# A hybrid encoder layer on one core: re-planned with a shared read port and measured step lengths, the last chunk's norms at once, first transfers in another sequence

## Chip, core and metric

One core of a Trainium2 chip runs one launch. The time is device time in microseconds of that core, 1225.96 us as the median of 3 runs of the kernel before. The engines are TensorE (PE; its weight loads are shown as PEld), VectorE (DVE), ScalarE (ACT), GpSimd (POOL) and SyncE (SP), which issues all transfers.

## The reference, cut to what matters

One layer is computed for 1024 prompt frames and 64 sample frames (1088 columns in all), with 1024 channels in f32. Only what carries time stands here.

```python
def _layer(h, ...):
    proj = _rmsnorm(h, pre_mix_g) @ w_in                     # 1024 x 2056
    z, xbc, dt_raw, u_pool = split(proj)
    xbc, new_conv = _causal_dwconv(xbc, conv_hist, conv_w, conv_b)   # width 4
    xs, bm, cm = split(silu(xbc))
    dt = softplus(dt_raw + dt_bias)
    y, new_ssm = _ssd_scan(xs, dt, -exp(a_log), bm, cm, ssm_h0)      # 8 heads
    y = (y + d_skip * xs) * silu(z)
    y = y * rsqrt(mean(y * y, per group) + EPS) * ssm_norm_g
    pool_out, new_pool = _multiscale_pool(u_pool, pool_hist, ...)    # windows 2, 4, 8, 16
    h = h + _rmsnorm(concat(y, pool_out) @ w_out, post_mix_g)
    hn = _rmsnorm(h, pre_ffn_g)
    f = (silu(hn @ w_gate) * (hn @ w_up)) @ w_down           # 2816 wide
    h = h + _rmsnorm(f, post_ffn_g)
    e = (p_i @ w_ple_proj) * sigmoid(h @ w_ple_gate)
    h = h + _rmsnorm(e, ple_norm_g)
```

## The kernel before, in words

The 1088 columns are cut into four chunks of 272 (`CH`, the last holds the sample frames too), and all activations lie with channels on the partitions. Each f32 operand of a large product is split into a high part rounded to fp32r (a cast on ACT) and a low part (the difference, on DVE, helper `sub`, L400); a product is then three fp32r matmuls of 272 columns: high x high, high x low, low x high (`PASSES`, helper `run`, L476). The stages follow each other on TensorE: the input projection with the convolution groups, the pooling groups and the gate (about 6 to 275 us), with the SSD scan's small matmuls in between; the output projection by chunks (to about 375); 32 small products of the per-layer input, the fills (372 to 401; L1801 is the ACT copy that frees their PSUM bank); the FFN in two phases, gate and up then down (401 to 1108, L1618); the input gate (to 1212); the tail. The FFN uses a seven-product block scheme: each operand exists in seven forms (`FORMS`), each form a cast on ACT (L1453, L1546) and a low part on DVE (L400). `hforms(p)` makes them for a pair of chunks p, from normed activations; `mixf` is the residual stream that it reads. A PSUM accumulation of the FFN ends in L1881 on DVE.

The order of all queues is written out by a planner while the program is built (`Layout`). Jobs are generators that yield a request: an engine letter, a length in us, and optionally a wait. "A" is ACT, "D" DVE, "G" POOL, "P" a small piece on TensorE, "S" SP. The planner keeps a time at which each engine comes free, gives the next place on an engine to the job that can start first (ties within 0.2 us by priority), and lets the clock run by the planned length of each matmul (`mmt`). TensorE's large products come in program order; the pieces "P" are put in where the planned time stands. A wait of 0, 1 or 2 means a hop of 0.2 us after the step before on another engine, TW means 0.04, and a number n from 3 on means n x 0.92 us. Transfers are planned at 500 or 680 columns per us. On the chip there is no planner: each engine runs its queue in order and waits on semaphores, so that a planned length only decides the order.

`rstd_job` (L497) makes 1/sqrt(mean + eps) for a chunk: eight one-column matmuls sum over the partitions (L511; twice the count in the trace's f32 passes), nine tiny DVE steps on 68 x 4 elements (L516 to L545) do the root, and four transposes bring the values back as a row in PSUM (L549):

```python
        f = 0 if fast else 1
        yield ("P", 0.52 * na, f)
        # L511, then L516 ("D", 0.16), then eight of ("D", 0.16, TW) up to L545
        yield ("P", 0.3 * na, 3 * f)
        # L549
```

`post_mix(c)` uses it twice for each output chunk: for the norm behind the output projection (tiles t_m), then `two(i)` scales pairs of channel blocks on DVE (L1402), adds x on POOL (L1408, `XM = 'GGGG'`) and squares (L601, sums L608 and L619), and again for the norm ahead of the FFN (tiles t_h), then `norm(m)` eight times on DVE (L1433). Neither was fast.

At the start, transfers are issued in this order: 8 parameter columns, the first half of input weight 0, x pieces of chunk 0 (piece 0), the dt weights (32 KB), the second half of weight 0, pieces 1 to 3, weight 1, the other 772 parameter columns (386 KB), weights 2 and 3, then chunk 1's pieces. A piece is two channel blocks k, 272 KB. `x_split` makes the high part on ACT (L731) and the low part on DVE (L733); `x_square` squares and adds for the norm, chunk 0 on POOL (L756). The first group of products runs by k (L914: high weight with both parts of x; L918: low weight). The dt products (L720) need `dt_w` (L815, L816) on DVE. `gt_job` (L841) multiplies four parameter columns on DVE; it is planned 10 x 0.92 us after the start, without a tie to the transfer:

```python
    def gt_job():
        yield ("D", 0.16, 10)
        ve.tensor_tensor(pcol("pool_b"), pcol("pool_b"), pcol("pool_scale"), ALU.mult)
```

## Time and profile before

| | |
|---|---|
| runs | 1224.27, 1225.96, 1226.66 us |
| profiled execution, its own time | 1226.61 us |
| its span, first to last instruction | 1224.8 us |
| mean granted TensorE clock | 0.993 |
| TensorE busy / weight loads | 1200.6 / 1180.8 us |
| DVE / ACT / POOL busy | 872.8 / 571.8 / 69.4 us |
| moved by DMA | 182.56 MB |

Times in the trace are microseconds from the first instruction. Busy time of TensorE counts matmuls as overlapping pipelines. An idle time is named by what released the engine; a wait on several semaphores is put down to the one that came last.

### The profile page before, as it was taken

Reading aid. Unit: us, or ns where it says so; the run is one execution under the profiler, and the core shown is the slowest. Engines: PE = TensorE matmul, PEld = TensorE weight load, DVE = VectorE, ACT = ScalarE, POOL = GpSimd, SP = SyncE. Lnnn points to the kernel's source line nnn. Section 1 sums busy time; section 2 is a strip of 40 time slices with the busy share of each in tenths; the row PEclk is TensorE's granted clock in tenths of the full one; section 3 lists DMA queues with packets and bytes.
Section 4 is the critical chain, followed back from the end, with each engine's and each line's share of the span. In section 5 each row is a group of like instructions: output and inputs, shape, how many; then the busy total and the mean of one; then the engine's idle time right before and its main releaser. Section 6 shows DMA issues by size and latency. Waiting matters only on the chain.

```text
span 1224.8 us, 23784 instructions
## 1 busy us (share of the span) xinstructions
PE 1200.6 (98%) x9641; PEld 1180.8 (96%) x9641; DVE 872.8 (71%) x1572; ACT 571.8 (47%) x1119; POOL 69.4 (6%) x56
## 2 busy tenths in 40 slices
PE   8999999999999999999999999999999999999997
PEld 6999999999999899999999999999999999999996
DVE  5697787874898776676677576766646655688875
ACT  6365557854456444443444444444432212356543
POOL 2000000120232000000000000000000000001111
PEclk8999999999999999999999999999999999999998
DMA  6122133243354144443443344336978676334422
GB/s 224 45 74 88 54 110 106 61 124 119 123 175 161 64 133 153 161 151 119 143 162 135 125 153 162 116 140 244 394 299 287 217 254 220 127 108 128 138 82 83
DMA packets 73777, 182.56 MB, mean 149 GB/s; under 512 B 8700, under 2 KB 17220, under 8 KB 73668
## 3 DMA queue, kind: packets, MB, share of 16 engines
q1 hardware_dynamic: 73668, 181.06, 42.9%
q8 instruction: 75, 1.23, 0.4%
q14 instruction: 34, 0.28, 0.1%
HBM read 122.03 MB, written 59.00 MB: 148 GB/s over the span
## 4 chain that ended last, share of the span: by engine, by line
PE 62%; DVE 3%; DMA 2%; POOL 0%; ACT 0%; issue 0%; DVEq 0%; ACTq 0%; POOLq 0%; SPq 0%
PE psall L1618 54%; PE psall L476 6%; PE psall L493 2%; DMA al_B<-af_dram 1%; POOL mixf L1408 0%; DMA raw_d<-in_wdn_dram 0%; DVE f L1881 0%; PE psall L511 0%; DMA raw_pg<-in_wpg_dram 0%; DVE mixf L1433 0%; DVE sq_f L608 0%; PE psall L549 0%; DMA e_dram<-e 0%; DVE mixf L1402 0%; DVE mixf L1465 0%
## 5 line engine op out<-in xcount | busy, mean ns | idle before, releaser
L476 PE MATMUL psall<-x,w_in 128*128 128x272 f32 x1440 | 193.8, 291 | 0.0
L476 PEld LDWEIGHTS psall<-x,w_in 128*128 128x128 f32 x1440 | 184.0, 188 | 3.3 <-issue 2.8
L1881 DVE TENSOR_TENSOR f<-f,psall 128x544 f32<-128x544 f32 (+1 forms) x96 | 60.7, 638 | 69.3 <-PE psall L1618 67.7
L1618 PE MATMUL psall<-h_T,w_g_S 128*128 128x272 f32 x792 | 102.9, 290 | 2.2 <-DVE h_T L400 1.8
L1618 PEld LDWEIGHTS psall<-h_T,w_g_S 128*128 128x128 f32 x792 | 101.1, 191 | 2.6 <-DVE h_T L400 2.0
L1618 PE MATMUL psall<-al_T,w_d_S 128*128 128x272 f32 x768 | 100.1, 289 | 1.0 <-ACT sq_f L601 0.5
L1618 PE MATMUL psall<-h_T,w_u_S 128*128 128x272 f32 x792 | 100.7, 287 | 0.0
L1618 PEld LDWEIGHTS psall<-h_T,w_u_S 128*128 128x128 f32 x792 | 99.6, 188 | 0.0
L1618 PEld LDWEIGHTS psall<-al_T,w_d_S 128*128 128x128 f32 x768 | 97.6, 188 | 1.7 <-ACT sq_f L601 0.7
L476 PE MATMUL psall<-mix,w_out 128*128 128x272 f32 x720 | 93.3, 289 | 0.0
L476 PEld LDWEIGHTS psall<-mix,w_out 128*128 128x128 f32 x720 | 90.9, 188 | 0.0
L1618 PE MATMUL psall<-al_B,w_d_A 128*128 128x272 f32 x528 | 72.1, 289 | 2.6 <-DVE w_d_A L400 2.6
L476 PE MATMUL psall<-h,w_pg 128*128 128x272 f32 x576 | 74.3, 289 | 0.0
L476 PEld LDWEIGHTS psall<-h,w_pg 128*128 128x128 f32 x576 | 72.7, 188 | 0.0
L1618 PEld LDWEIGHTS psall<-al_B,w_d_A 128*128 128x128 f32 x528 | 68.4, 188 | 3.1 <-DVE w_d_A L400 3.1
L1618 PE MATMUL psall<-h_B,w_g_A 128*128 128x272 f32 x528 | 70.2, 288 | 0.1
L1618 PE MATMUL psall<-h_B,w_u_A 128*128 128x272 f32 x528 | 69.7, 288 | 0.0
L1618 PEld LDWEIGHTS psall<-h_B,w_g_A 128*128 128x128 f32 x528 | 67.7, 188 | 0.3 <-ACT e L1801 0.3
L1618 PEld LDWEIGHTS psall<-h_B,w_u_A 128*128 128x128 f32 x528 | 67.5, 188 | 0.0
L1546 ACT CAST w_d_A<-raw_d 128x512 fp32r<-128x512 f32 (+3 forms) x44 | 22.3, 523 | 69.9 <-PE psall L1618 35.1
L1546 ACT CAST w_d_S<-raw_d 128x512 fp32r<-128x512 f32 (+3 forms) x54 | 26.5, 532 | 57.7 <-DVE raw_d L1570 33.9
L2067 POOL TENSOR_TENSOR f<-f,sq_f 128x544 f32<-128x544 f32 x5 | 7.4, 1479 | 726.8 <-DVE f L2064 721.3
(401 smaller groups left out, 2246.0 us busy)
## 6 DMA issues: line engine op xcount, KB each, us to landing
af_dram<-a_T SPq DMA_DIRECT2D x88, 272.0 KB, 2.3
al_T<-af_dram SPq DMA_DIRECT2D x44, 544.0 KB, 5.6
af_dram<-a_B SPq DMA_DIRECT2D x66, 272.0 KB, 2.2
al_B<-af_dram SPq DMA_DIRECT2D x33, 544.0 KB, 5.9
raw_g<-in_wff_dram SPq DMA_DIRECT2D x22, 512.0 KB, 4.1
raw_u<-in_wff_dram SPq DMA_DIRECT2D x22, 512.0 KB, 3.7
raw_in<-in_wmix_dram SPq DMA_DIRECT2D x15, 512.0 KB, 3.8
raw_d<-in_wdn_dram SPq DMA_DIRECT2D x14, 512.0 KB, 5.3
```

The source lines that it names most:

```text
L476: pe.matmul(out, lhsT, rhs, start=i == 0, stop=i == n - 1)
L493: pe.matmul(out, w.v(wi, k), act.v(xi, k, L), start=first and n == 0, stop=not left and n == 2)
L1546: ac.copy(v[:, 0], src)
L1618: pe.matmul(d[:, p - q.ps[0], :], w.v(wi, k), u.b(bf, xi, p, k), start=start and not k and not wi and not xi, stop=k == u.ks - 1 and wi == ...
L1881: ve.tensor_tensor(v[:, sl], v[:, sl], src[:, pl], ALU.add)
L2067: gp.tensor_tensor(v, v, hr, ALU.add)
```

## The change

Part 1: `FAST_M` and `FAST_H` name chunk 3, whose two calls of `rstd_job` in `post_mix` are now fast. Part 2: the first transfers. Chunk 0's pieces 0 and 1 stand between the halves of weight 0; the dt weights come behind all of chunk 0; chunk 1's pieces 0 and 1 come behind weight 1, and the parameters behind weight 2. Part 3: the planner has a new letter "E" for DVE steps that read two tensors in SBUF; E and G steps don't overlap in the plan. Steps get other lengths. `mmt` goes from 14 to 12 added columns, and a weight is given back after its own last group. `dma_add` and the branches for "A" are new, but no letter in `XM` or `XF` is "A" (`XM, XF = 'GGGG', 'GDGD'`).

```diff
+FAST_M, FAST_H = (3,), (3,)
...
+        self.port = {"E": 0.0, "G": 0.0}
...
-                if callable(req) or req[0] not in self.busy:
+                if callable(req) or req[0] not in "ADEG":
                     continue
-                start = max(job["ready"], self.busy[req[0]])
+                start = max(job["ready"], self.busy["D" if req[0] == "E" else req[0]])
+                if req[0] in "EG":
+                    start = max(start, self.port["G" if req[0] == "E" else "E"])
...
+            if eng in "EG":
+                self.port[eng] = start + cost
+            if eng == "E":
+                eng = "D"
...
-        return (1.0625 * n + 14) / 2400
+        return (1.0625 * n + 12) / 2400
...
-        xr0 += [x_dma(C0, k2) for k2 in ((0,), (1, 2, 3))[h]]
-        if not h:
-            dt_at = dma(wdr, wdt, NK * 8)
+        xr0 += [x_dma(C0, k2) for k2 in ((0, 1), (2, 3))[h]]
+    dt_at = dma(wdr, wdt, NK * 8)
...
-    dma(cp[:, PFIRST:], par[:, PFIRST:], PWIDTH - PFIRST)
+    xr1 = [x_dma(ORD_X[1], k2) for k2 in range(2)]
     for i in (2, 3):
+        if i == 3:
+            dma(cp[:, PFIRST:], par[:, PFIRST:], PWIDTH - PFIRST)
...
     def x_job():
+        for k2 in range(2):
+            x_spawn(ORD_X[1], k2, *xr1[k2], P_XP)
         for c in ORD_X[1:]:
-            for k2 in range(4):
+            for k2 in range(2 if c == ORD_X[1] else 0, 4):
...
             conv_group(i, c, getw(f"in{i}"), i == 0)
-    for i in range(4):
-        donew(f"in{i}")
+            if c == ORD_X[-1]:
+                donew(f"in{i}")
...
-        yield from rstd_job(ss.halves(), L, 1024.0, f"m{c}", flag, free=ss.free)
+        yield from rstd_job(ss.halves(), L, 1024.0, f"m{c}", flag, fast=c in FAST_M, free=ss.free)
...
-            yield from rstd_job(ss2.halves(), L, 1024.0, f"h{c}", got, free=ss2.free)
+            yield from rstd_job(ss2.halves(), L, 1024.0, f"h{c}", got, fast=c in FAST_H, free=ss2.free)
```

The lengths that differ most (us before and after; the letter E where a second SBUF operand is read):

```diff
-            yield ("D", 1.0, 0)
+            yield ("D", 0.72, 0)
...
-                yield ("G", 1.6, at)
+                yield ("G", 1.35, at)
...
-            yield ("A", 0.78, 1)
+            yield ("A", 1.0, 1)
...
-                yield ("D", 1.06)
+                yield ("E", 1.29)
...
-            yield ("A", 0.24, 0)
+            yield ("A", 0.38, 0)
...
-                yield ("A", 0.48, 1)
+                yield ("A", 0.39, 1)
...
-                yield ("D", 0.8)
+                yield ("E", 0.72)
```

In order these are: the scaling by rstd in `two(i)` (L1402, and L2064 behind the FFN), the residual addition on POOL (L1408), the cast and the low half of an FFN operand form (`hforms`), the d_skip scaling in `ssd`, the fills' copy (L1801), and the sum of squares (L608).

## Rows read from the trace of the kernel before

**Rows 1.** Part 1 of the page: engine, busy us (share of the span), instructions.

```profile
PE 1200.6 (98%) x9641; PEld 1180.8 (96%) x9641; DVE 872.8 (71%) x1572; ACT 571.8 (47%) x1119; POOL 69.4 (6%) x56
```

**Rows 2.** The span cut into stretches of 25 us; the line names the stretch and its length, then each engine's busy us (and instructions), the granted TensorE clock, the DMA engines' busy share and GB/s.

```profile
50.00:75.00 25.00, 25.00 (x210) 24.96 (x209) 17.66 (x37) 11.74 (x17) 0.00 (x0) 1.00 0.07 22
375.00:400.00 25.00, 22.64 (x181) 21.74 (x181) 21.85 (x43) 15.22 (x35) 7.43 (x4) 1.00 0.48 174
```

**Rows 3.** What TensorE (PE) waited for, over the whole span: waiting line <- releasing line: us in total, times, longest us. Five of seventeen rows, and the last of them.

```profile
PE psall L1618 <- DVE w_d_A L400: 2.6, 2, 1.4
PE psall L476 <- ACT e L1801: 2.3, 3, 0.9
...
PE psall L1618 <- DVE h_T L400: 1.8, 1, 1.8
...
PE psall L1618 <- DVE f L1881: 1.5, 3, 0.5
...
PE psall L493 <- DVE h L400: 1.2, 2, 0.8
...
PE psall L1224 <- DVE pl L400: 0.2, 1, 0.2
```

**Rows 4.** The order of time from 380 to 425 us: start us, us, engine, line, operation, out<-in, operand shapes, count of the merged instructions, and in brackets the idle time before and its releaser. Chunk 3's m norm (t_m) and h norm (t_h).

```profile
381.68 0.60 PE L511 MATMUL psall<-cp,xr 128*68 128x1 f32 x8
...
383.94 0.16 DVE L545 SCALAR_TENSOR_TENSOR t_m<-t_m 68x4 f32<-68x4 f32 x1
...
388.70 0.40 PE L549 MATMUL psall<-cp,t_m 68*128 68x68 f32 x4
...
389.99 5.08 POOL L1408 TENSOR_TENSOR mixf<-mixf,sq_m 128x544 f32<-128x544 f32 x3 [23.75 <-DVE mixf L1402]
...
395.02 2.41 POOL L1408 TENSOR_TENSOR mixf<-mixf,xr 128x544 f32<-128x544 f32 x1
...
401.54 0.60 PE L511 MATMUL psall<-cp,p 128*68 128x1 f32 x8
...
403.80 0.16 DVE L545 SCALAR_TENSOR_TENSOR t_h<-t_h 68x4 f32<-68x4 f32 x1
...
406.98 0.40 PE L549 MATMUL psall<-cp,t_h 68*128 68x68 f32 x4
...
416.24 0.39 PE L1618 MATMUL psall<-h_T,w_g_S 128*128 128x272 f32 x1 [0.38 <-ACT h_T L1453]
...
418.45 6.04 PE L1618 MATMUL psall<-h_T,w_g_S 128*128 128x272 f32 x35 [1.83 <-DVE h_T L400]
```

**Rows 5.** Three neighbouring stretches of equal length around the last wait of the group above; columns as in Rows 2.

```profile
414.70:418.10 3.40, 1.54 (x11) 1.12 (x9) 3.40 (x5) 2.30 (x3) 0.00 (x0) 1.00 0.00 0
418.10:421.50 3.40, 3.04 (x13) 3.05 (x14) 3.05 (x4) 0.38 (x2) 0.00 (x0) 0.50 0.00 0
421.50:424.90 3.40, 3.40 (x29) 3.40 (x28) 2.13 (x2) 2.94 (x5) 0.00 (x0) 1.00 0.00 0
```

**Rows 6.** The order of time from 374 to 381 us, columns as in Rows 4: chunk 2's h norm (t_h), and a form that DVE makes in between.

```profile
374.71 0.65 PE L511 MATMUL psall<-cp,sq_m 128*68 128x1 f32 x8
...
378.46 1.28 DVE L400 TENSOR_TENSOR h_T<-mixf,h_T 128x1088 fp32r<-128x1088 f32 x1
...
380.24 0.16 DVE L545 SCALAR_TENSOR_TENSOR t_h<-t_h 68x4 f32<-68x4 f32 x1
```

**Rows 7.** The order of time of TensorE at the start, columns as in Rows 4; the last row is from 29 to 31 us.

```profile
8.95 1.58 PE L914 MATMUL psall<-x,w_in 128*128 128x272 f32 x4 [1.81 <-ACT x L731]
...
10.60 2.04 PE L720 MATMUL psall<-xraw,wd 128*32 128x272 f32 x16
...
15.92 0.79 PE L476 MATMUL psall<-x,w_in 128*128 128x272 f32 x5
...
29.83 0.51 PE L493 MATMUL psall<-x,w_in 128*128 128x272 f32 x2 [0.47 <-DVE x L733]
```

**Rows 8.** The start again, columns as in Rows 4: the cast of the first weight's second half and the splits of x behind it on ScalarE (ACT), the issue of the third and fourth weight on SP, and two DVE rows; then the transfer that was issued at 5.45 alone: engine, operation, count, KB, us from issue to landing.

```profile
5.45 1.95 SPq L382 DMA_DIRECT2D raw_in<-in_wmix_dram  x2
...
7.35 0.62 ACT L827 CAST w_in<-raw_in 128x512 fp32r<-128x512 f32 x1 [1.20 <-DMA raw_in<-in_wmix_dram]
...
8.37 0.93 ACT L731 ACTIVATE x<-xraw,cp 128x272 fp32r<-128x272 f32 x2
...
12.12 0.72 DVE L841 TENSOR_TENSOR cp<-cp 128x4 f32<-128x4 f32 x1
...
12.89 1.23 DVE L400 TENSOR_TENSOR w_in<-raw_in,w_in 128x1024 fp32r<-128x1024 f32 x1
...
raw_in<-in_wmix_dram SPq DMA_DIRECT2D x1, 512.0 KB, 7.9
```

**Rows 9.** Two neighbouring stretches of the start; columns as in Rows 2.

```profile
8.50:11.90 3.40, 2.88 (x16) 1.60 (x20) 3.16 (x9) 3.40 (x10) 0.92 (x2) 0.50 1.02 404
11.90:15.30 3.40, 3.40 (x20) 2.73 (x13) 2.35 (x4) 3.40 (x8) 3.24 (x3) 0.50 1.04 414
```

**Rows 10.** Lines by the tiles that they write: duration in ns, least, median and most, first and last start in us, shapes. POOL's additions (whole span), the low halves of the FFN's operand forms on DVE (372 to 425); and, as line, operation, tiles, shapes and count | busy us, mean ns | idle time before, their casts on ScalarE (372 to 402).

```profile
L1408 POOL TENSOR_TENSOR mixf<-mixf,sq_m x9: 1357/1378/2424, 315.9 to 392.6; 128x544 f32<-128x544 f32 x9
...
L400 DVE TENSOR_TENSOR h_B<-mixf,h_B x4: 1282/1526/2433, 380.7 to 424.0; 128x1088 fp32r<-128x1088 f32 x4
...
L1453 ACT CAST h_B<-mixf 128x1088 fp32r<-128x1088 f32 x3 | 3.3, 1105 | 0.6 <-DVE mixf L1433 0.6
```

More of the change, by code (lines that the diff above doesn't have):

```diff
@@ L250, in step @@
             wait = req[2] if len(req) > 2 else 0
-            job["ready"] = max(job["t"] + (HOP if req[0] != job["eng"] else HOPS), wait) if isinstance(wait, At) else job["t"] + (0.04 if wait == TW else wait * self.PIECE if wait >= 3 else HOP if req[0] != job["eng"] else HOPS)
+            eng = "D" if req[0] == "E" else req[0]
+            job["ready"] = max(job["t"] + (HOP if eng != job["eng"] else HOPS), wait) if isinstance(wait, At) else job["t"] + (0.04 if wait == TW else wait * self.PIECE if wait >= 3 else HOP if eng != job["eng"] else HOPS)
         return True
@@ L383, in dma, with dma_add @@
         return lay.load(cols)
+    def dma_add(dst, src, cols):
+        gp.dma_start(dst, src, accum_op=ALU.add)
+        return lay.load(cols)
     cp = const.tile([P, PWIDTH], F32, name="cp")
@@ L447, in gen @@
             ac.copy(w.t[0], raw)
-            yield ("D", 1.23)
+            yield ("E", 1.23)
             sub(ve, w.t[1], raw, w.t[0])
@@ L1394, in two @@
         def two(i):
-            yield n2.ok
-            xr = n2.take(f"xr{c}_{i}")
-            yield ("S", 0, 0)
-            at = dma(xr, xT[c][:, 2 * i:2 * i + 2], 2 * L)
+            if XM[i] != "A":
+                yield n2.ok
+                xr = n2.take(f"xr{c}_{i}")
+                yield ("S", 0, 0)
+                at = dma(xr, xT[c][:, 2 * i:2 * i + 2], 2 * L)
             yield lambda: bool(flag)
             v = mf[i // 2][:, i % 2 * 2:i % 2 * 2 + 2, :]
-            yield ("D", 1.0, 0)
+            yield ("D", 0.72, 0)
             ve.tensor_tensor(v, v, flag[0][:, :L].unsqueeze(1).broadcast_to([P, 2, L]), ALU.mult)
@@ L2057, in two @@
                 ac.activation(v[:, q], v[:, q], AF.Identity, scale=pcol("post_ffn_g", 2 * i + q))
-            yield n2.ok
-            hr = n2.take(f"hr{c}_{i}")
-            yield ("S", 0, 0)
-            at = dma(hr, h1_d[c][:, 2 * i:2 * i + 2], 2 * L)
+            if XF[i] != "A":
+                yield n2.ok
+                hr = n2.take(f"hr{c}_{i}")
+                yield ("S", 0, 0)
+                at = dma(hr, h1_d[c][:, 2 * i:2 * i + 2], 2 * L)
             yield lambda: bool(flag)
-            yield ("D", 1.0, 0)
+            yield ("D", 0.72, 0)
             ve.tensor_tensor(v, v, flag[0][:, :L].unsqueeze(1).broadcast_to([P, 2, L]), ALU.mult)
-            if XF[i] == "G":
-                yield ("G", 1.6, at)
+            if XF[i] == "A":
+                yield ("S", 0, 0)
+                yield ("S", 0, dma_add(v, h1_d[c][:, 2 * i:2 * i + 2], 2 * L))
+            elif XF[i] == "G":
+                yield ("G", 1.35, at)
                 gp.tensor_tensor(v, v, hr, ALU.add)
             else:
-                yield ("D", 0.73, at)
+                yield ("E", 0.73, at)
                 ve.tensor_tensor(v, v, hr, ALU.add)
-            n2.give(hr)
+            if XF[i] != "A":
+                n2.give(hr)
             hi, lo = (H2[c].pages[s_][i // 2][:, i % 2 * 2:i % 2 * 2 + 2] for s_ in range(2))
@@ L2074, in two @@
             ac.copy(hi, v)
-            yield ("D", 0.73)
+            yield ("E", 0.72)
             sub(ve, lo, v, hi)
```

66 lines of the change are left out of this document (35 added, 31 removed).

## The prediction

> **What bounds the kernel now.** I read the page's busy times first, then the stretches of 25 us, then the list of what TensorE waited for, then the order of time around the longest waits, and at last the clock and the transfers there. The reader is to see that TensorE is busy for 98% of the span and DVE for 71% [rows 1], and that most 25 us stretches, as 50 to 75, hold no TensorE idle time at all [rows 2]. What can be won is what TensorE loses in a few places: the start, the stretch from 372 to 421 where the last output chunk is normed and the FFN begins, a weight at 883 and 900, the end of the FFN, and the tail. The list of waits has seventeen rows, from 2.6 us down to 0.2, some 19 us together; those that this change can reach [rows 3] are 2.6 us for low weight halves at 883 and 900, 2.3 for the copies of the projection fills, 1.8 for one low half of an FFN operand, 1.5 for accumulations and 1.2 for the last operands. So a re-laid order has little to win and, since the rest is dense, much room to lose.
>
> **Part 1: the last chunk's norms.** `rstd_job` sums on TensorE (L511), runs nine tiny DVE steps (L516 to L545) and transposes back (L549). Without `fast` the plan places the transposes 3 x 0.92 = 2.76 us after the last tiny step, with it 0.2 us, so 2.56 earlier. For chunk 3 the trace shows more than the planned delay [rows 4]: the m norm's values were ready at 383.94 + 0.16 = 384.10 and its transposes ran at 388.70, 4.6 later; the h norm's were ready at 403.96 and transposed at 406.98, 3.0 later. Behind the first stand the scaling on DVE, four POOL additions (5.08 + 2.41 us), squares and the next sums at 401.54; behind the second stand eight norm steps and the FFN's operand forms, one of whose low halves (L400) releases TensorE at 418.45. That whole chain comes forward by 2 x 2.56 = 5.1 us at least in the plan, by 7.6 at most.
> TensorE's loss at the end of the chain is 0.38 + 1.83 us of waiting [rows 4], and a clock that fell after it: the granted clock was 0.50 of full speed, 1.2 GHz, from 418.1 to 421.5, with 13 matmuls started there against 29 in the next equal stretch [rows 5]. 16 matmuls of 3.40 / 29 = 0.117 us are 1.9 us; 0.36 of it is idle time already counted (3.40 - 3.04), which leaves 1.5. Together 0.38 + 1.83 + 1.5 = 3.7 us. The need is for 2 us, the chain gains 5 or more, so all of it goes. Next late behind it is the up-projection's first weight, with no wait in the rows.
> The price: the transposes now stand in TensorE's queue close behind their sums, and everything behind them waits if DVE is late. Planned from the start of L511 they come after 0.52 + 0.36 + 8 x 0.2 + 0.2 = 2.7 us. For chunk 3 DVE took 384.10 - 381.68 and 403.96 - 401.54, both 2.4 us; for chunk 2's h norm it took 380.24 + 0.16 - 374.71 = 5.7, because a 1.28 us form and others stood in front [rows 6]. So each of the two costs between 0 and 3.0 us; I take 0.2, by the rows of chunk 3 itself. Sum of part 1: -3.7 + 0.4 = -3.3, with ends -4.5 (all, and 0.8 of the fills' waits) and +2.3 (6.0 - 3.7).
>
> **Part 2: the first transfers.** The second piece of x now stands before the second half of the first weight and the 32 KB of dt weights behind all of x; chunk 1's first two pieces stand before the third weight, and the 386 KB of parameters behind it. Before, TensorE waited 1.81 us for x until 8.95, then did the dt products (16 in 2.04 us), which filled the time until k = 4 to 7 were split, and reached the second weight at 15.92 [rows 7]. The second piece now lands about when the weight's half did, which released ScalarE's cast at 7.35, rather than before its own splits at 8.37 [rows 8], so k = 2 and 3 come 1 us sooner or a little more. But the weight's half then lands at 8.4, the later pieces no sooner, and the dt products wait for a transfer that is now eighth: the 1.81 us of waiting moves to k = 4 more than it goes. From 8.5 to 15.3 the clock was granted at 0.50 [rows 9]. I take 0.4 us for it, and 0.4 for chunk 1's splits, whose 0.47 us wait at 29.83 [rows 7] loses its cause when two pieces land early.
> Against it stands L841, a DVE step of 4 columns on the parameters, which the plan places at a fixed time. It ran at 12.12, just before the low half of the second weight (12.89 to 14.12) [rows 8]. The parameters now come behind 544 KB of x and 512 KB of weight that followed them. The third weight landed at 5.45 + 7.9 = 13.35 [rows 8] and the fourth, 512 KB at some 0.41 MB a microsecond [rows 9], at an estimated 14.6; the bytes up to the end of the parameters are now, within 32 KB, those up to the end of the fourth weight before, so they land at about 14.7. DVE stands until then, and the second weight's low half is ready at 14.7 + 0.1 + 1.23 = 16.0 instead of 14.1. TensorE needs it 16 matmuls, 2.0 us, after it starts this weight, at 17.9 or a little earlier: hidden at half clock, up to 1.5 us of waiting if the start got quicker. Part 2: -0.8, ends -3.1 (the whole 2.3 of the rival below and 0.8) and +1.5.
>
> **Part 3: lengths and the port.** No instruction is added, removed or lengthened; the plan alone sees other costs, and DVE steps with two SBUF operands (E) and POOL steps exclude each other in it. The rows agree with that: a POOL addition takes 1.36 us undisturbed and up to 2.42, an operand form on DVE 1.28 and up to 2.43 [rows 10]. The new lengths are nearer to the rows (casts 1.11 us, planned 0.78 before and 1.0 now; forms 1.28, planned 1.06 and 1.29). What that moves is the order in five queues, at the places where TensorE waits at all; I cannot follow it instruction by instruction. I take 0 of the fills' 2.3, the 2.6 at 883 and 900, and the 2.7 of L1881 and L493 near the end, with bounds of -3 (some 40% of these 7.6) and +3, as much the other way. Where TensorE has no idle time [rows 2] there are 25 - 17.66 = 7 us of free DVE in such a stretch, which hides a changed order. The Trainium skill, page SBUF — State Buffer, section "SBUF: two separate sides", speaks against a gain here: it says that whichever engine starts first keeps the shared pair for its whole instruction, so that a planned order holds only if the engines keep the planned times. By that the four additions of the chain stay at 7.5 us as in the trace, and by a plan that holds they would take 5.4; the sum is the same, since the chain has spare time. Giving `in0` back after its own last group frees its pages 9 us earlier (three groups of 24 matmuls), where no weight is waited for: 0. The branch for "A" is never taken.
>
> **Sum.** -3.3 - 0.8 + 0 = -4.1 on the profiled execution's 1226.61 us: 1222.5. That execution stands 0.65 above the median of the runs, 1225.96, so the forecast is 1221.9.
>
> **Rivals.**
> (a) The start's clock rises sooner. If TensorE, fed with k = 2 and 3 a microsecond earlier, is back at full speed by 11.9, the products at half clock [rows 9] shrink to the pace of the inputs: k = 7 is split when DVE goes on to L841, at 12.1 [rows 8], then 8 products of 0.117 us and the second half of dt (half of 1.02) take 1.5 us, and the second weight begins at 13.6, not 15.92. That is 2.3 instead of 0.4: 1220.0. Against it: the wait moves to k = 4. The Trainium skill, TensorE: Matmul & The Clock Gate, section "Part 1: The HAM clock gate", has the slow clock as the state at rest and activity as what ends it; with the same idle time in another place that leaves the start as it was.
> (b) The norms come earlier and TensorE waits in the fills instead. In 375 to 400 it waits for copies that ScalarE makes one behind the other [rows 2, 3]; three 1.11 us casts of operand forms now fall there. As waiting that is 3.3 us, all that part 1 brings: 1221.9 + 3.3 = 1225.2. For it: ScalarE is in order and no other work fills; against it: ScalarE is busy 15.2 of those 25 us.
> (c) Slower: both fast transposes meet a DVE as far behind as in chunk 2 [rows 6]. 2 x 3.0 us, and 1.5 for a clock that falls behind such a wait, instead of 0.4: 1221.9 + 7.1 = 1229.0. It decides from 4.5 us of added waiting on. For it: the h norm moves to about 396, where DVE has forms and squares; against: both of chunk 3's own chains took 2.4 us.
>
> **How the numbers follow.** Forecast 0.50 (its own range 1219.5 to 1223.5), (a) 0.11, (b) 0.22, (c) 0.17, in which I count other orders of part 3 that go wrong. About 0.2%, 2.45 us, is what a measurement can tell from no change: faster is below 1223.5, slower above 1228.4. Nearly all of the forecast and (a) is faster, (b) the same, (c) slower but for its cheaper half: 0.61, 0.22, 0.17. The range 1216.5 to 1228.5 takes in part 3's gain on top of the forecast below, and (b) and half of (c) above.
>
> **What would show it.** Right: L549 of chunk 3 within 0.5 us behind its L545, the next sums before 398, no wait at L1618 between 401 and 425 and a clock at 1.00 there; L841 behind a transfer that lands after 14. Wrong: a wait of more than 1 us at either L549 or at L1801's copies; or a start that reaches the second weight by 14, or later than 16.5.

## The result, and the profile after

The changed kernel runs in 1227.93 us (median of its runs; 1224.93 for the kernel before on the same chips). The ratio is 1.0018, 95% interval 1.0011 to 1.0026: about 2 us slower, where 4 us faster was forecast. The ratio is that of the means of the fast runs (one of the change's 20, of 1457.15 us, is left out); the medians lie 3.0 us apart. The profiled execution took 1227.99 us, its span is 1226.2 (1224.8 before). Line numbers have moved by 16 to 24: L511, L545, L549 are now L527, L561, L565; L400 is L416, L1402 and L1408 are L1422 and L1431, L1618 is L1642, L841 is L858.

First the busy times of the page, which answer to [rows 1]:

```profile
PE 1201.8 (98%) x9641; PEld 1181.8 (96%) x9641; DVE 862.6 (70%) x1572; ACT 577.0 (47%) x1123; POOL 65.2 (5%) x56
```

Nothing is to be seen there: TensorE has the same 9641 instructions and 1.2 us more busy time. The stretches of 25 us, and then two of 3.4 us (columns as in rows 2), answer to [rows 2, 5]:

```profile
375.00:400.00 25.00, 25.00 (x212) 25.00 (x211) 21.71 (x48) 17.05 (x38) 5.34 (x4) 1.00 0.60 213
400.00:425.00 25.00, 20.05 (x140) 19.40 (x139) 20.13 (x35) 9.94 (x17) 0.00 (x0) 0.86 0.00 1
...
416.00:419.40 3.40, 2.96 (x13) 2.96 (x14) 3.39 (x4) 0.38 (x2) 0.00 (x0) 0.50 0.00 0
419.40:422.80 3.40, 3.40 (x18) 3.40 (x18) 2.04 (x2) 2.32 (x3) 0.00 (x0) 0.57 0.00 0
```

The stretch 375 to 400 has lost all its idle time (22.64 us busy before, 25.00 now), and the next has it: 20.05 busy, at a mean granted clock of 0.86. In the two stretches from 416.0 to 422.8 the granted clock was 0.50 and 0.57 of full speed, 1.2 GHz nearly throughout; before, it was so in one such stretch [rows 5]. The list of TensorE's waits answers to [rows 3]:

```profile
PE psall L1642 <- DVE h_T L416: 2.9, 1, 2.9
PE psall L1642 <- DVE w_d_A L416: 2.6, 2, 1.4
PE psall L1642 <- DVE f L1905: 2.4, 4, 0.9
...
PE psall L1642 <- DVE xr L1685: 1.7, 1, 1.7
...
PE psall L509 <- ACT h L2103: 0.7, 1, 0.7
```

The waits for the fills' copies (L1801 before) are gone from the list. In their place stand 2.9 for a low half of an FFN operand and 1.7 for an accumulation just before it; 2.6 for the down-projection's weights is unchanged, and the accumulations at the FFN's end cost 2.4 instead of 1.5. From the first down-projection matmul to the first matmul of the last projection, before and then after (columns as in rows 2):

```profile
862.53:1108.63 246.10, 241.33 (x1910) 239.41 (x1909) 160.97 (x281) 78.80 (x147) 1.36 (x1) 1.00 0.65 232
861.74:1109.66 247.92, 242.32 (x1910) 239.64 (x1909) 161.30 (x282) 79.12 (x148) 1.36 (x1) 1.00 0.64 230
```

This stretch is 1.8 us longer now, at the full clock both times. The order of time from 380 to 425 shows where the waits come from; it answers to [rows 4]:

```profile
383.44 0.60 PE L527 MATMUL psall<-cp,sq_m 128*68 128x1 f32 x8
...
386.18 0.16 DVE L561 SCALAR_TENSOR_TENSOR t_m<-t_m 68x4 f32<-68x4 f32 x1
...
387.83 0.40 PE L565 MATMUL psall<-cp,t_m 68*128 68x68 f32 x4
...
389.12 1.37 POOL L1431 TENSOR_TENSOR mixf<-mixf,xr 128x544 f32<-128x544 f32 x1 [21.41 <-DVE mixf L1422]
...
390.43 1.39 POOL L1431 TENSOR_TENSOR mixf<-mixf,sq_m 128x544 f32<-128x544 f32 x1
...
391.75 2.71 POOL L1431 TENSOR_TENSOR mixf<-mixf,xr 128x544 f32<-128x544 f32 x2
...
394.06 1.81 DVE L624 TENSOR_TENSOR p<-p,sq_m 128x544 f32<-128x544 f32 x2
...
395.66 0.67 ACT L617 ACTIVATE xr<-mixf 128x544 f32<-128x544 f32 x1
395.79 1.28 DVE L416 TENSOR_TENSOR h_B<-mixf,h_B 128x1088 fp32r<-128x1088 f32 x1
...
396.27 3.18 PE L1642 MATMUL psall<-h_B,w_g_A 128*128 128x272 f32 x24
396.99 0.72 DVE L624 TENSOR_TENSOR p<-p,xr 128x544 f32<-128x544 f32 x1
397.62 1.28 DVE L416 TENSOR_TENSOR h_B<-mixf,h_B 128x1088 fp32r<-128x1088 f32 x1
...
398.83 0.43 DVE L635 TENSOR_TENSOR p<-p 128x272 f32<-128x272 f32 x1
...
400.41 0.60 PE L527 MATMUL psall<-cp,p 128*68 128x1 f32 x8
...
403.07 0.16 DVE L561 SCALAR_TENSOR_TENSOR t_h<-t_h 68x4 f32<-68x4 f32 x1
...
403.96 0.40 PE L565 MATMUL psall<-cp,t_h 68*128 68x68 f32 x4
...
409.54 1.79 PE L1642 MATMUL psall<-h_B,w_g_S 128*128 128x272 f32 x12 [1.74 <-DVE xr L1685]
...
416.44 7.29 PE L1642 MATMUL psall<-h_T,w_g_S 128*128 128x272 f32 x35 [2.85 <-DVE h_T L416]
```

Read down this list beside [rows 4]. The FFN's first product starts at 396.27, 4.8 us earlier than before (401.06). But chunk 3's chain (sums, tiny steps, transposes, scaling, additions, squares, sums, tiny steps, transposes) is hardly earlier: the m sums stand at 383.44, 1.8 later than before; the h sums at 400.41, 1.1 earlier; the last transposes at 403.96, 3.0 earlier. Three delays can be read off. The m transposes (387.83) come 1.5 us behind their values (386.18 + 0.16). The last square leaves ScalarE at 396.33 (395.66 + 0.67), but a form that started on DVE at 395.79 runs to 397.07, and a second one from 397.62 to 398.90 stands ahead of the last sum (398.83, overlapping by a few hundredths). And the h sums wait from 399.26 to 400.41 in TensorE's queue behind FFN products. After that TensorE stands for 1.74, 0.37 and 2.85 us, 4.96 in all. The up-projection begins at 423.57 against 424.33: of the 4.8 us won, 0.8 is left, and that 0.8 stood already at the last output matmul (371.20 before, 370.44 now). So the stretch from there to the up-projection takes 53.1 us both times: against the kernel before nothing is won in it, and what the change is slower by lies behind it. The two spans are 1.4 us apart: 0.8 less before the last output matmul, 1.8 more at the FFN's end, 0.4 more from the last projection on.

The start, in order of time, answers to [rows 7 to 9]:

```profile
8.13 0.62 ACT L844 CAST w_in<-raw_in 128x512 fp32r<-128x512 f32 x1 [1.09 <-DMA raw_in<-in_wmix_dram]
...
9.55 2.92 PE L933 MATMUL psall<-x,w_in 128*128 128x272 f32 x8 [1.53 <-ACT x L747]
...
14.62 0.34 DVE L858 TENSOR_TENSOR cp<-cp 128x4 f32<-128x4 f32 x1 [2.13 <-DMA cp<-in_par_dram]
...
14.88 1.21 DVE L416 TENSOR_TENSOR w_in<-raw_in,w_in 128x1024 fp32r<-128x1024 f32 x1
...
16.27 0.54 PE L492 MATMUL psall<-x,w_in 128*128 128x272 f32 x3
```

The cast of the first weight's second half came at 8.13 instead of 7.35, behind the second piece of x. The parameters' step L858 stood for 2.13 us until they landed at 14.62, the low half behind it was ready at 16.09 (14.88 + 1.21), and the second weight began at 16.27 instead of 15.92.

### The profile page after: what moved, and what is told of

Read it like the earlier page. It is cut to its first block, busy times and chain, and to the rows that moved or that the text cites. A ratio compares the mean times of both kernels' runs of the same rounds, so it can differ in the third digit from the quotient of the medians.

```text
span 1226.2 us, 23743 instructions
## 1 busy us (share of the span) xinstructions
PE 1201.8 (98%) x9641; PEld 1181.8 (96%) x9641; DVE 862.6 (70%) x1572; ACT 577.0 (47%) x1123; POOL 65.2 (5%) x56
## 4 chain that ended last, share of the span: by engine, by line
PE 92%; DVE 3%; ACT 2%; DMA 1%; issue 1%; SPq 0%; DVEq 0%; ACTq 0%
PE psall L1642 55%; PE psall L492 29%; PE psall L509 2%; PE psall L527 1%; PE psall L1128 1%; PE psall L565 1%; PE psall L1157 1%; PE psall L1122 1%; DVE f L1905 0%; DMA raw_in<-in_wmix_dram 0%; PE psall L1243 0%; PE psall L736 0%; DMA raw_out<-in_wout_dram 0%; DVE w_out L416 0%; DMA raw_pg<-in_wpg_dram 0%
## 5 line engine op out<-in xcount | busy, mean ns | idle before, releaser
L1642 PE MATMUL psall<-h_T,w_g_S 128*128 128x272 f32 x792 | 104.4, 292 | 3.2 <-DVE h_T L416 2.9
L1642 PEld LDWEIGHTS psall<-h_T,w_g_S 128*128 128x128 f32 x792 | 102.5, 193 | 3.6 <-DVE h_T L416 3.1
L1642 PE MATMUL psall<-al_T,w_d_S 128*128 128x272 f32 x768 | 100.4, 289 | 1.4 <-DVE f L1905 0.9
L1642 PE MATMUL psall<-h_T,w_u_S 128*128 128x272 f32 x792 | 100.8, 287 | 0.0
L1642 PEld LDWEIGHTS psall<-al_T,w_d_S 128*128 128x128 f32 x768 | 97.7, 188 | 2.3 <-ACT w_pg L463 0.9
L1642 PEld LDWEIGHTS psall<-h_T,w_u_S 128*128 128x128 f32 x792 | 99.6, 188 | 0.0
L1642 PE MATMUL psall<-al_B,w_d_A 128*128 128x272 f32 x528 | 72.3, 289 | 2.7 <-DVE w_d_A L416 2.6
L1642 PEld LDWEIGHTS psall<-al_B,w_d_A 128*128 128x128 f32 x528 | 68.5, 188 | 3.3 <-DVE w_d_A L416 3.1
L1642 PE MATMUL psall<-h_B,w_g_A 128*128 128x272 f32 x528 | 69.9, 288 | 0.0
L1642 PE MATMUL psall<-h_B,w_u_A 128*128 128x272 f32 x528 | 69.8, 288 | 0.0
L1642 PEld LDWEIGHTS psall<-h_B,w_u_A 128*128 128x128 f32 x528 | 67.7, 188 | 0.0
L1642 PEld LDWEIGHTS psall<-h_B,w_g_A 128*128 128x128 f32 x528 | 67.6, 188 | 0.0
L416 DVE TENSOR_TENSOR w_u_S<-raw_u,w_u_S 128x512 fp32r<-128x512 f32 x44 | 30.3, 688 | 26.5 <-ACT w_u_S L1570 26.4
```

Of the source, the lines that this page charges most:

```text
L416: eng.tensor_tensor(lo, src, hi.bitcast(F32), ALU.subtract)
L1642: pe.matmul(d[:, p - q.ps[0], :], w.v(wi, k), u.b(bf, xi, p, k), start=start and not k and not wi and not xi, stop=k == u.ks - 1 and wi == ...
```

## The experiments

All ratios are to the kernel before, run on the same chip; 0.1% is 1.2 us. Two quantities are read from each trace in the order of time: **T**, from the start of the last output-projection matmul to that of chunk 3's last transposes, and **S**, from the same start to the up-projection's first matmul.

| kernel | ratio [interval] | T, us | S, us |
|---|---|---|---|
| before | 1 | 35.8 | 53.1 |
| the change | 1.0018 [1.0011, 1.0026] | 33.5 | 53.1 |
| p1_fast_alone | 0.9958 [0.9944, 0.9971] | 29.5 | 46.8 |
| p2_transfers_alone | 0.9999 [0.9990, 1.0007] | 35.8 | 53.3 |
| p3_plan_alone | 1.0063 [1.0050, 1.0076] | 39.1 | 57.1 |
| after_no_fast | 1.0060 [1.0048, 1.0073] | 39.1 | 57.2 |
| after_no_port | 1.0011 [0.9998, 1.0023] | 30.2 | 47.5 |
| after_old_lengths | 1.0062 [1.0047, 1.0077] | 35.7 | 54.2 |
| after_forms_no_port | 1.0000 [0.9990, 1.0010] | 32.9 | 49.2 |
| after_matmul_14 | 0.9996 [0.9986, 1.0006] | 31.7 | 50.2 |
| part1_port | 1.0078 [1.0063, 1.0092] | 35.9 | 53.2 |
| part1_matmul_12 | 1.0030 [1.0020, 1.0041] | 31.8 | 48.2 |
| part1_forms_port | 0.9955 [0.9942, 0.9969] | 29.8 | 47.0 |
| part1_forms_lengths | 0.9958 [0.9945, 0.9970] | 31.3 | 47.5 |
| after_forms_old_lengths | 0.9980 [0.9970, 0.9989] | 30.1 | 47.4 |
| part1_m_only | 0.9962 [0.9949, 0.9975] | 32.2 | 48.5 |
| after_two_adds_dve | 1.0030 [1.0018, 1.0042] | 35.0 | 53.5 |
| part1_and_2 | 0.9945 [0.9932, 0.9957] | 29.5 | 46.8 |

**Each part alone, and the change without part 1.**

p1_fast_alone is the kernel before with `fast` in chunk 3's two calls of `rstd_job`, p2_transfers_alone the kernel before with the change's transfers; p3_plan_alone is the change with the old transfers and the second edit below, after_no_fast the change with that edit alone.

```diff
@@ p1_fast_alone @@
+FAST_M, FAST_H = (3,), (3,)
...
-        yield from rstd_job(ss.halves(), L, 1024.0, f"m{c}", flag, free=ss.free)
+        yield from rstd_job(ss.halves(), L, 1024.0, f"m{c}", flag, fast=c in FAST_M, free=ss.free)
...
@@ p3_plan_alone, after_no_fast @@
-FAST_M, FAST_H = (3,), (3,)
+FAST_M, FAST_H = (), ()
```

> The kernel before with part 1 alone (chunk 3's two norms fast). Theory A (TensorE's second half of the first FFN pass waits for chunk 3's chain of norm and operand forms, and only an earlier end of that chain is time won): the chain ends 4 to 5 us earlier than 418.45, the waits of 0.38 + 1.83 us and the slow clock go, 2 to 4 us faster than before. Rival B (the transposes make TensorE wait as long as they bring): within 1 us of before, with waits of 1 us or more at L549-like lines.

> The kernel before with part 2 alone (first transfers). Theory A: the DVE step on the parameters waits some 2 us for its transfer, as in the changed kernel (2.13), and TensorE reaches the second weight 0 to 0.5 us later; the whole within 1 us of before. Rival C (the start costs what the changed kernel lost): 2 us slower.

> The kernel before with part 3 alone (port, lengths, matmul length, earlier give-back). Theory A: TensorE comes to the FFN 3 to 5 us earlier because the fills no longer wait, and waits that much longer for chunk 3's chain, whose end moves little; the end of the FFN loses 1.5 us as in the changed kernel: 1 to 4 us slower than before. Rival D (the plan is what the fills' 2.3 us need and nothing takes it back): 2 us faster.

> The changed kernel with neither norm of chunk 3 fast. Theory A: chunk 3's chain ends 3 to 5 us later than 416.4 and TensorE waits for all of it: 2 to 5 us slower than the changed kernel, so 4 to 7 slower than before. Rival B: no slower than the changed kernel.

Measured: 1219.39, 1224.51, 1232.41 and 1232.48 us. Part 1 alone wins 0.42%, part 2 nothing that can be told (-0.10% to +0.07%), part 3 alone loses 0.63%; the sum, +0.20%, is the change's +0.18% within the intervals. So the parts add up, and part 3 turned a gain into a loss. Part 1 won more than theory A had said (2 to 4 us) and part 3 lost more (1 to 4). Part 1 alone, in order of time:

```profile
380.67 0.60 PE L513 MATMUL psall<-cp,xr 128*68 128x1 f32 x8
...
383.80 0.40 PE L551 MATMUL psall<-cp,t_m 68*128 68x68 f32 x4
...
396.55 0.60 PE L513 MATMUL psall<-cp,p 128*68 128x1 f32 x8
...
399.72 0.40 PE L551 MATMUL psall<-cp,t_h 68*128 68x68 f32 x4
...
404.75 1.78 PE L1620 MATMUL psall<-h_T,w_g_S 128*128 128x272 f32 x12 [0.42 <-ACT xr L1658]
...
416.94 3.17 PE L1620 MATMUL psall<-h_B,w_u_A 128*128 128x272 f32 x24
```

Its m sums stand 10.5 us behind its last output matmul (370.18), as before (371.20 to 381.68), where the change has 13.0 (370.44 to 383.44). The last transposes come at 399.72, 1.9 us after the FFN's start (397.85); from there on the only wait before the up-projection is 0.42, and the up-projection begins at 416.94. Part 3 alone, over the same events:

```profile
395.95 3.19 PE L1639 MATMUL psall<-h_B,w_g_A 128*128 128x272 f32 x24
...
400.21 0.43 DVE L635 TENSOR_TENSOR p<-p 128x272 f32<-128x272 f32 x1
...
402.73 0.60 PE L527 MATMUL psall<-cp,p 128*68 128x1 f32 x8
...
408.18 0.40 PE L565 MATMUL psall<-cp,t_h 68*128 68x68 f32 x4
...
417.71 0.60 PE L1639 MATMUL psall<-h_T,w_g_S 128*128 128x272 f32 x1 [7.19 <-ACT h_T L1474]
...
420.31 4.90 PE L1639 MATMUL psall<-h_T,w_g_S 128*128 128x272 f32 x26 [2.01 <-DVE h_T L416]
```

The last sum is there at 400.64 (400.21 + 0.43), and TensorE takes it up at 402.73, 2.1 us later, since FFN products stand in front; the transposes come 3.1 us behind their values, and the two waits are 7.19 and 2.01 us.

**A delay in front of the FFN.** Ten more f32 matmuls (some 4.6 us), whose output nobody reads, stand ahead of the FFN's first product and are unknown to the plan.

```diff
+for _ in range(10):
+    pe.matmul(psall[:, banks.order[0], :CW], ident, cp[:, :CW], start=True, stop=True)
```

> The changed kernel with 10 more f32 matmuls (identity by 272 parameter columns, result unused) on TensorE between the fills and the FFN, some 4.6 us, that the plan does not know. Theory A (TensorE waits there for chunk 3's chain anyway, 5 us, and its clock falls): 0 to 2 us faster, never more than 0.5 slower, because the clock need not fall. Rival B (TensorE's own work sets the time): 4.6 us slower.

> Part 1 alone with the same 10 matmuls in the same place. Theory A: there TensorE hardly waits for the chain (0.6 us), so the 4.6 us are paid: 4 to 5 us slower than part 1 alone, 1223 to 1224.5. Rival B: the same here.

Measured: 1232.84 and 1224.19, ratios 1.0062 [1.0047, 1.0077] and 0.9990 [0.9981, 1.0000]. In the change the delay should have disappeared in the 4.96 us of waiting; it was paid in full (0.44%), as it was in most part in part 1 (0.32%). The trace shows why: the h sums moved from 400.41 to 404.50 and the transposes from 403.96 to 408.05, and the waits stayed 1.74, 0.38 and 2.84. S grew from 53.1 to 56.6 us, in part 1 from 46.8 to 51.3. The chain's own pieces stand in TensorE's queue behind the delay, so TensorE and chain are late together. My first theory, that the chain ran on DVE and POOL alone and TensorE only came too early for it, fell here.

**Which edit of part 3.** First the port rule and the lengths, each taken out of the change as a whole; of the many lengths one is shown.

```diff
@@ after_no_port @@
-                if req[0] in "EG":
-                    start = max(start, self.port["G" if req[0] == "E" else "E"])
@@ after_old_lengths @@
-                yield ("E", 1.29)
+                yield ("E", 1.06)
```

> The changed kernel with the new lengths, but without the rule that E and G steps exclude each other in the plan. Theory A1 (the port rule in the plan pushes DVE's and POOL's work on chunk 3 back, which costs the 7.7 us of the plan alone): 4 to 8 us faster than the changed kernel, so 2 to 5 faster than before. Theory A2 (the new lengths cost it): within 2 us of the changed kernel.

> The changed kernel with the port rule, but with the lengths of before at every step. Theory A1: within 2 us of the changed kernel. Theory A2: 4 to 8 us faster than the changed kernel. If both halves are needed for the loss, both kernels come near part 1 alone, 1219 to 1221.

Measured: 1226.58 and 1233.19. Without the rule S falls to 47.5, nearly that of part 1 alone; but the last output matmul comes at 374.5 instead of 370.4, the last projection takes 1.7 us longer (105.1 instead of 103.3), and what S won is lost again. With the old lengths under the rule both get worse, which neither theory had said. The order of DVE in the change suggested the next theory, called A from here on: the rule holds the FFN's operand forms (`hforms`) back behind POOL's additions, and they then take DVE ahead of the chain. So the forms were taken out of the rule, and the planned cost of a matmul was set back; and each edit was put on top of p1_fast_alone, part1_port with the whole rule at the old lengths.

```diff
@@ after_forms_no_port @@
-                yield ("E", 1.29)
+                yield ("D", 1.29)
@@ after_matmul_14 @@
-        return (1.0625 * n + 12) / 2400
+        return (1.0625 * n + 14) / 2400
@@ part1_port @@
+        self.port = {"E": 0.0, "G": 0.0}
...
+                if req[0] in "EG":
+                    start = max(start, self.port["G" if req[0] == "E" else "E"])
@@ part1_matmul_12 @@
-        return (1.0625 * n + 14) / 2400
+        return (1.0625 * n + 12) / 2400
```

> The change with one edit: the plan places the FFN operand forms' steps of `hforms` as plain DVE steps, so it no longer holds them back while POOL adds (all lengths as in the change, the port rule kept everywhere else). Theory A: the port rule piles these 1.28 us forms up behind POOL's additions, where they take DVE ahead of chunk 3's last square sums; chunk 3's m sums then come by 382.2 (383.44 in the change), its last transposes by 401 (403.96), the waits of 1.74, 0.37 and 2.85 us before the up-projection shrink below 1.5 us together, the up-projection begins by 420.5 (423.57) and the median is 1223 to 1225, some 3 to 4 us under the change. Rival L: the longer planned lengths do it, not the port; then the waits stay at 4 us or more and the median at 1227 to 1229. Rival Q: TensorE is only earlier at the chain's end and any order costs the same; then the transposes come earlier, but the time goes into other waits before 426 and the median stays within 1 us of the change.

> The change with the planned cost of a matmul back at 14 cycles of overhead instead of 12. By theory A (port rule and operand forms) this is not the cause: the waits at the FFN's start stay at 3 us or more together, with 1226 to 1231. Rival M: with 12 the plan thinks TensorE earlier than it is by 0.8 ns a matmul, 2 to 3 us by the FFN's start, and lays chunk 3's sums behind more FFN matmuls; then with 14 the h sums stand before the FFN's first matmul or less than 1 us behind it, the waits fall below 1.5 us, and the median is below 1225.

> Part 1 (the fast norms) with the port rule alone on top: DVE steps with two SBUF operands and POOL steps exclude each other in the plan, with all lengths, the matmul cost, the transfers and the place of donew as before. Theory A: the loss comes with the rule: waits of 2 us or more together between 400 and 425 and a median of 1223 to 1228 (part 1 alone: 1219.4). Rival L: the rule alone costs nothing, 1218.5 to 1221, and the loss is the lengths'.

> Part 1 with the planned matmul overhead at 12 cycles, and nothing else of part 3. Theory A: no loss at the FFN's start, waits there below 1 us together, 1218 to 1221.5. Rival M: 12 cycles lay chunk 3's pieces behind FFN matmuls: waits of 2 us or more there and 1223 to 1227.

Measured: 1224.39, 1224.46, 1234.48 and 1228.74. The first came out as theory A said for the waits (1.2 us left) and the median, not for the chain: m sums still at 383.64, transposes at 402.28. The second speaks against A: 0.22% went with a matmul cost alone, though 3.2 us of waits stayed. Both edits also hurt part 1, by 1.2% and 0.7%, more than any of the theories had said, and there somewhat under half of it is lost before the last output matmul (376.7 and 374.1 against 370.2); in S it is 6.4 and 1.4 us, and part1_matmul_12 loses 2.8 more in the last projection (106.2 against 103.4). Last, each edit of the forms by itself:

```diff
@@ part1_forms_port, with the rule as in part1_port @@
-                yield ("D", 1.06)
+                yield ("E", 1.06)
@@ part1_forms_lengths @@
-            yield ("A", 0.78, 1)
-                yield ("D", 1.06)
+            yield ("A", 1.0, 1)
+                yield ("D", 1.29)
@@ after_forms_old_lengths @@
-            yield ("A", 1.0, 1)
-                yield ("E", 1.29)
+            yield ("A", 0.78, 1)
+                yield ("E", 1.06)
```

> Part 1 (the fast norms) with the port rule for the FFN operand forms of `hforms` alone: those two kinds of DVE step and POOL's steps exclude each other in the plan, at the old lengths; every other DVE step is planned as before. Up to the first of these forms the order is that of part 1 alone. Theory A (the forms pile up behind POOL's additions and take DVE ahead of chunk 3's squares): the stretch from the last output matmul to the up-projection grows from 46.8 us (part 1 alone) to 50 us or more, with waits of 2 us or more together there, and the median goes from 1219.4 to 1222.5 to 1227. Rival L (the lengths do it): the stretch stays at 46 to 48 us and the median at 1218.5 to 1221.

> Part 1 with the planned lengths of the FFN operand forms alone as in the change (casts 0.78 to 1.0, DVE steps 1.06 to 1.29), without the port rule. Theory A: the stretch from the last output matmul to the up-projection stays at 46 to 49 us and the median at 1218.5 to 1222. Rival L: the stretch grows to 50 us or more, and the median to 1222.5 to 1227.

> The change with the operand forms' old planned lengths (casts 0.78, DVE steps 1.06), the port rule kept. Theory A: the stretch from the last output matmul to the up-projection stays at 51 us or more (53.1 in the change) and the median at 1226 to 1230. Rival L: the stretch falls to 49 us or less and the median below 1225.

Measured: 1219.37, 1220.04 and 1222.58. Neither edit costs anything on top of part 1, against theory A; taking the lengths out of the change wins 0.38%, against A again; and the same lengths cost nothing alone, against L. So no single edit of those tried is the culprit. What the slow orders share is a late chain, T, though T does not say all: after_forms_no_port has a T of 32.9 against 33.5 in the change, and an S of 49.2 against 53.1.

**The chain by itself.** One kernel delays chunk 3's h transposes in the fastest order, one shortens the chain in the change.

```diff
@@ part1_m_only @@
-FAST_M, FAST_H = (3,), (3,)
+FAST_M, FAST_H = (3,), ()
@@ after_two_adds_dve @@
+        xm = "GGDD" if c == 3 else XM
...
-            if XM[i] == "A":
+            if xm[i] == "A":
...
-            elif XM[i] == "G":
+            elif xm[i] == "G":
```

> Part 1 for the m norm alone: chunk 3's h norm keeps its transposes 2.76 us behind the last tiny step. In the runs so far the stretch from the last output matmul to the up-projection goes with the time of chunk 3's last transposes (29.5 us after the last output matmul and 46.8 us long with part 1, 33.5 and 53.1 in the change, 39.1 and 57.1 with part 3 alone). Theory C (this chain sets the stretch): the transposes come 32 to 33.5 us after the last output matmul, the stretch is 48.5 us or longer, and the median 1221 to 1224 (part 1: 1219.4). Rival: the stretch is set elsewhere (TensorE's own work, weights); then it stays at 46.5 to 47.5 us and the median at 1218.5 to 1220.5.

> The change with two of chunk 3's four POOL additions on DVE, everything before them in the same order: the chain between chunk 3's two norms gets shorter by about two additions of 1.36 us less 0.73 us of DVE work. Theory C: the last transposes come 1.5 to 3 us earlier than 33.5 us after the last output matmul, the stretch falls from 53.1 to 48 to 51 us, and the median from 1227.9 to 1223 to 1226. Rival: DVE is what is full there, and its two more steps push the operand forms back; the stretch stays at 52.5 us or more.

The first, 1220.91 us; in order of time:

```profile
397.31 0.60 PE L513 MATMUL psall<-cp,p 128*68 128x1 f32 x8
...
403.12 0.40 PE L551 MATMUL psall<-cp,t_h 68*128 68x68 f32 x4
...
411.24 1.77 PE L1620 MATMUL psall<-h_B,w_g_S 128*128 128x272 f32 x12 [1.31 <-DVE sq_m L1663]
...
414.85 4.75 PE L1620 MATMUL psall<-h_T,w_g_S 128*128 128x272 f32 x35 [0.20 <-DVE h_T L402]
```

TensorE reached the FFN's first product 27.7 us after the last output matmul, as in part 1. The transposes are 5.2 us behind the end of the sums instead of 2.6, T is 32.2 and S 48.5, at the edge of what theory C said; 1.31 us of wait is back and the clock stayed at 1.00. The ratio, 0.9962, can't be told from part 1's 0.9958, so the trace shows this effect and the times don't settle it. The second, 1228.77 us:

```profile
396.82 0.72 DVE L624 TENSOR_TENSOR p<-p,xr 128x544 f32<-128x544 f32 x1
397.46 2.49 DVE L416 TENSOR_TENSOR h_B<-mixf,h_B 128x1088 fp32r<-128x1088 f32 x2
...
399.87 0.44 DVE L635 TENSOR_TENSOR p<-p 128x272 f32<-128x272 f32 x1
...
401.65 0.60 PE L527 MATMUL psall<-cp,p 128*68 128x1 f32 x8
...
405.20 0.40 PE L565 MATMUL psall<-cp,t_h 68*128 68x68 f32 x4
```

Here the rival held. The additions were over by 392.80 instead of 394.46, but now two forms in a row (2.49 us) stand between the last square's addition and the last sum, which ends at 400.31 instead of 399.26, and TensorE takes it up at 401.65 instead of 400.41. T grew to 35.0, S only to 53.5. What delays the chain in both kernels is the place of its short steps behind forms on DVE and behind products on TensorE; shorter additions alone did not help.

**The version the runs point to.** Parts 1 and 2 without part 3.

```diff
@@ before @@
+FAST_M, FAST_H = (3,), (3,)
...
-        xr0 += [x_dma(C0, k2) for k2 in ((0,), (1, 2, 3))[h]]
-        if not h:
-            dt_at = dma(wdr, wdt, NK * 8)
+        xr0 += [x_dma(C0, k2) for k2 in ((0, 1), (2, 3))[h]]
+    dt_at = dma(wdr, wdt, NK * 8)
...
```

> The version the runs point to: parts 1 and 2 of the change without part 3, that is the kernel before with the fast norms of chunk 3 and the new sequence of first transfers. Theory A (the parts add up, part 2 is worth nothing): 1218.5 to 1221, 4 to 6 us faster than before, within 0.1% of part 1 alone. Rival S: part 2 moves the plan of all that follows, and with it chunk 3's place, so that 2 us or more of part 1's gain go: 1221.5 or above.

Measured: 1218.23 us, 0.55% (0.43 to 0.68) faster than before, the fastest kernel of the study; against part 1 alone (0.9958) the intervals overlap.

## Why the prediction was wrong

**The step that failed is part 3**: "I take 0 of the fills' 2.3, the 2.6 at 883 and 900, and the 2.7 of L1881 and L493 near the end, with bounds of -3 (some 40% of these 7.6) and +3". Alone it cost 0.63%, 7.7 us, more than twice the upper bound; on top of parts 1 and 2 it cost 0.73% (1.0018 against 0.9945), 9 us. The bound counted TensorE's present waits at a few places and assumed that as much could be added there. Most of the loss came at a place that is not among them, the FFN's start: its waits grew from 2.2 us [rows 4] to 9.2 (7.19 and 2.01) in part 3 alone. In the profile of part 3 alone, S is 4.0 us longer; the FFN's first phase from the up-projection on 0.5; from the first down-projection matmul to the first of the last projection it takes 247.9 us instead of 246.1, and from there on 0.4 more. The last output matmul came 2.1 us earlier there, of which 1.0 stands also in part 1's trace, whose start is coded as before: executions differ by so much at the start. (The two profiled executions, 1231.46 and 1226.61, lie only 4.9 us apart, as that of before stands above its median and that of part 3 below; the 7.7 is the ratio's.) The same account for the change against part1_and_2, spans 1226.2 and 1216.5: 1.1 us before the last output matmul, 6.4 in S, 1.9 at the FFN's end, 0.4 from the last projection on. The 1.8 us at the FFN's end come with all of part 3 and not with part 1 or 2 (246.0 to 246.1). On part 1, the rule alone (246.1), the forms' lengths alone (246.1) and the matmul cost alone (246.4) do not bring them either, while every kernel that keeps two or more of the three, the rule, the new lengths and the matmul cost, has 247.1 to 248.7 there. Why stays open.

**The second failure is a sentence beside it**, "the sum is the same, since the chain has spare time". In the change the four additions took 5.34 us (389.12 to 394.46), just what "a plan that holds" would give, since the forms stand behind them. That the rule did this is not shown: in part 1 alone, planned without the rule, they took 5.36 (385.30 to 390.66). In the change the forms then stand at the chain's next steps. What the Trainium skill says on the page SBUF — State Buffer, section "SBUF: two separate sides", that whichever engine starts first keeps the shared pair, agrees with the rows: 1.37 us for an addition now, 2.41 for the one beside a form before [rows 4, 10]. Obeying it in the plan was no gain: TensorE's waits there are not for the additions but for what came behind them.

**Part 1** was right in kind and too small: -3.3 forecast, 0.42% (5.1 us) measured alone, and as much in the change (1.0060 without, 1.0018 with). Of its terms, the 3.7 us of waits and clock measured 4.2 (FFN start 3.2 us earlier, up-projection 7.4 earlier, in part 1's trace); the fills, for which only the lower end had 0.8, gave 2.2 (last output matmul to FFN start 27.7 us instead of 29.9). That the trace gives 6.4 and the ratio 5.1 has a reason: the profiled execution of before, 1226.61 us, stands 2.0 above the median of the runs beside part 1 (1224.65). The price of 0.4 was about right: in part 1 the last transposes came 0.75 us behind their values, nothing waited. In the change the forecast signs were all absent: transposes 1.5 and 0.7 us behind L561 instead of 0.5, the next sums at 400.41 instead of before 398, 4.96 us of waits at L1642. The signs of being wrong were absent too (no wait at either L565 or for the copies, the second weight at 16.27): the forecast looked for trouble at the transposes and the copies, not at the steps between. "The need is for 2 us, the chain gains 5 or more" failed in the change on both sides: TensorE came 4.8 us earlier, the chain gained 3.0. In part 1 alone it held: 3.2 and 7.3.

**Part 2** was forecast at -0.8 and measured 0.9999 alone; the interval, 0.9990 to 1.0007, is -1.2 to +0.9 us and can't tell -0.8 from 0. Its mechanism was right in each step: the wait for x moved (1.81 before, 1.53 at k = 4 now), L858 stood for the parameters until 14.62 (14.7 forecast), the low half was ready at 16.09 (16.0). Whether the 0.4 for the start failed can't be read from single profiles: in the two stretches of [rows 9] the clock was granted at 0.50 and 0.50 before and at 0.82 and 0.68 in part 1 alone, whose start is coded as before, and the second weight began at 15.92 and 14.86; with the new transfers it began at 16.27 in the change, 14.80 in p2_transfers_alone and 15.15 in part1_and_2. The wait of 0.47 for chunk 1's x is gone in the last two, 0.32 is left in the change. The lower end, -3.1, counts the start's 0.4 twice; its terms give -2.7.

**The rivals.** (a) did not happen: none of these starts reached the second weight by 13.6. (b) had it the wrong way round: the fills' waits went to nothing and came back behind them. (c), the only slower one, named another mechanism: both of the change's own norms took 2.9 and 2.8 us on DVE (383.44 to 386.34, 400.41 to 403.23), 0.5 more than before, not 3. (Its 4.5 us of added waiting should be 5.4 by its own terms: 1221.9 + 5.4 + 1.5 - 0.4 = 1228.4.) That part 1's gain could go again along this same chain was in its reach; the cause, steps of the chain ordered behind forms and products, stood in no rival.

**What is shown and what stays open.** That part 3 turned the gain into a loss is shown by the parts alone and by part1_and_2. That its order loses in S because the chain stands late is shown by the table, where S follows T (T runs from 29.5 to 39.1, S - T stays within 16.2 and 19.6), and by part1_m_only, which moved only chunk 3's h transposes in the plan: T grew by 2.7 us, S by 1.8, with TensorE at the FFN no later. after_two_adds_dve moved T by 1.5 and S by only 0.3. What T does not say is mostly the clock. From the FFN's first product to the up-projection, in before, the change and part 1 alone (columns as in rows 2):

```profile
401.06:424.33 23.27, 21.06 (x156) 20.55 (x157) 17.02 (x31) 11.24 (x20) 0.00 (x0) 0.93 0.11 38
396.27:423.57 27.30, 22.35 (x159) 21.70 (x157) 22.75 (x38) 12.11 (x24) 0.00 (x0) 0.87 0.12 42
397.85:416.94 19.09, 18.67 (x150) 18.45 (x149) 17.58 (x29) 10.87 (x19) 0.00 (x0) 1.00 0.15 51
```

In the nine rows of the table in which the clock stayed at 1.00 here, S - T is 16.2 to 17.3; in the nine in which it fell, 17.3 to 19.6, the most in the change. Of the 8.2 us that the change takes longer here than part 1, 4.5 are waits (4.96 against 0.42), and an estimated 2.7 the clock: in its two stretches at 0.50 and 0.57, 31 matmuls started against 58 at the pace of [rows 5], and 27 of 0.117 us are 3.2 us, less 0.4 of idle time already counted. Against the kernel before, the change's chain is earlier (T 33.5 against 35.8), but TensorE came to the FFN earlier still, waited longer and at a lower clock, and S stayed the same. Why just these planned costs lay the steps so, why half of part 3 loses 3 to 6 us before the last output matmul (at 373.7 to 376.7 in after_no_port, after_old_lengths, part1_port and part1_matmul_12), and what costs 1.8 us at the FFN's end, stays open.

## What to carry to other kernels

Where a plan orders in-order queues, better lengths are not a cost of zero: follow the one serial chain that the next dense stage needs, and look which long steps the new order puts ahead of its short ones, on every engine it visits. A gain of the busy engine just in front of such a chain is worth at most as much as the chain comes forward. Measure a bundle's parts alone: here one part won 5 us and another lost 8.

## What the runs showed of the hardware

The granted clock fell where TensorE stood longest: it was at 0.50 and 0.57 in the stretches from 416.0 to 422.8, behind waits of 1.74, 0.37 and 2.85 us in the change, and stayed at 1.00 through one of 1.31 and 0.20 in part1_m_only. The waits alone do not fix what it costs: with the same three waits (1.74, 0.38 and 2.84) in after_pad the mean from the FFN's first product to the up-projection was 0.94, against 0.87 in the change. A delay of 4.6 us on a TensorE that waits 5 us a little later was paid in full (+0.44%; S grew by 3.5 us in the profiles), since what it waits for passes through its own queue.
